# One encoder layer in full precision: the window of held operations opens at step 3, with a margin on TensorE

## The chip, the core and the metric

The kernel runs on one core of a Trainium2 chip. The core has five engines that each work through their own instruction stream in order: TensorE (PE: matmuls, and transposes done as matmuls), VectorE (DVE), ScalarE (ACT), GpSimd (POOL) and SyncE (SP, which here only issues DMAs). They wait for each other through semaphores. The metric is the time of one execution on the device, in microseconds.

## What is computed

One layer of a bidirectional encoder over 256 tokens with 4096 columns, in float32:

```python
h = rms_norm(x, g_mix)
proj = h @ w_in                      # 4096 x 11840: latents, rotary key, gates, q, k, v
y_a = mla_attention(...)             # 16 heads, low-rank q and kv, rotary part, dense softmax
y_b = dilated_mixture_attention(...) # 16 heads, three dilated windows with ALiBi, merged
x = x + concat(rms_norm(y_a, g) * silu(gate_a), rms_norm(y_b, g) * silu(gate_b)) @ w_out
x = x + (p @ w_ple) * sigmoid(rms_norm(x, g_ple) @ w_ple_gate)
out = rms_norm(x, g_final)
```

Nearly all of the work is five products of the 256 tokens with weights of 4096 rows (`w_in`, `w_out`, `w_ple_gate`) or fewer (`w_uq`, `w_ukv`). The weights are read once, about 365 MB.

## The kernel before

**Precision.** PE works on fp32r operands. To keep float32's precision each operand is split in a rounded part and a remainder: `hi` is a copy by ACT that rounds, `lo = src - hi` a subtraction by DVE (`split`, L415). A product is then three matmuls, hi x hi, hi x lo and lo x hi (`mm`, L433), accumulated in one PSUM bank. So each 512 KB piece of weights costs a load (SP), one ACT instruction, one DVE instruction and twelve matmuls of 512 columns.

**Steps.** The long products are cut into steps, one per 128 rows of weights and 1024 columns (`plain_step`), with some steps replaced by a Strassen-like scheme that forms sums of weights on DVE and saves one product in eight (`fast_steps`, letters a, b, g, h of `ORDER_*`). A step loads its weights into one of four raw slots, splits them into one of three pairs `hi`, `lo` (pool `wp`, and other tiles where they are free), and issues its matmuls into the eight PSUM banks m0 to m3, s, o, t0, t1. The main loop (L2232) goes through all steps: hooks, loads for some steps ahead (`fetch`), splits ahead (`convert`), the step's matmuls (`step.run`), and between them pieces of other tasks (`advance`): attention heads (`attend`), transposes of x, statistics, the epilogues of each product.

**The opening.** x comes in 512-column blocks (`load_x`, order 4, 5, 6, 7, 0 to 3). `x_turn` transposes a 128-token, 256-column piece on PE, and ACT and DVE scale it by the norm's gain and split it into `Ah`/`Al` (tiles A..h, A..l). Before the loop the program issues six small matmuls on a tile of zeros (`warm_up`), the transpose of the gains, the transposes of x block 8 into banks s and o (`x_turn(8, first)`), three more warm-up matmuls, and the splits of steps 0 and 1. Step 0 takes its weights in two halves; `blk.front` puts the split of its own piece of x ahead of the split of its weights. In step i of the first fifteen after step 0, `x_bank((i + 8) % 16)` transposes and splits the next piece of x, ahead of that step's matmuls.

**What sets the order.** All calls on an engine go through `Metered` (L253), which reckons a duration and hands the operation to two models. `clock` (class `Clock`) is a model of the engines in program order; the program asks it what to do next, and the change doesn't touch it. `window` (class `Window`, L179) holds operations back and issues them in another order: an operation is open when everything it depends on inside the window has been issued (`push`, L190); `step` (L221) takes for each engine the open operations that could start within `near` = 0.15 us of the earliest start by the window's own clock, and of these the first in program order; of the engines' candidates it issues the one that starts first. SP and POOL are kept in program order (`FIFO`). The window holds up to 200 operations:

```python
HELD = 200, 0.15                                              # L36
window = Window(*HELD)                                        # L327
at = max(free, min(op.at for op in ops))                      # L226
op = min((op for op in ops if op.at <= at + self.near), key=lambda op: op.nr)
```

`op.at` is the time at which the operation's operands are ready by the model. Operations are thus issued in an order fixed when the program is built; on the chip, every engine then follows its own list and waits wherever the next one isn't ready. Two matmuls that write overlapping parts of a PSUM tile keep their order by the dependency rule in `push`; two that write different parts of one tile (the transposes of one `tp`, the two halves of `s`) could be swapped.

All instructions are recorded at line 290, the helper that issues them, so the profile's groups are told apart by the names of tiles: m, s, o, t are the PSUM banks, `hi`, `lo` the split weights, `B`, `T`, `Ah`, `Al` tiles with several uses, `raw_all` the raw weights.

Of the kernel before, what the change touches and what calls it, by code (L numbers as in the profile page):

```python
# [32 lines left out]
SLOPES = [2.0 ** (-8.0 * (h + 1) / HEADS) for h in range(HEADS)]  # L33
FAR = 1e32
WARM = 6, 3
HELD = 200, 0.15  # L36
ORDER_D = (
    "cccccccccccccccccaccccbccccgchcccc",
    "ccccaabcbcgcgchhcaabbggcahchbagchbghcabgacbghhcc",
# [139 lines left out]
class Window:  # L179
# [10 lines left out]
    def push(self, engine, us, outs, ins, late, do, reads):  # L190
        op = Op(self.nr, engine, us, outs, ins, late, do)
        self.nr += 1
        first = set()
        if engine in self.FIFO and not getattr(self.tail.get(engine), "gone", True):
            first.add(self.tail[engine])
        self.tail[engine], op.gone = op, False
        for aps, wrote in ((reads, False), (outs, True)):
            for ap in aps:
                name, lo, hi = Clock.place(ap)
                both = wrote or ap.space == bass.MemoryType.PSUM  # L200
                for other, a, b, w in self.held.get(name, ()):
                    if (both or w) and a < hi and lo < b:
                        first.add(other)
                op.spans.append((name, lo, hi, both))
        for name, *span in op.spans:
            self.held.setdefault(name, []).append((op, *span))
        first.discard(op)
        op.before = len(first)
        for other in first:
            other.then.append(op)  # L210
        self.n += 1
        if not op.before:
            self.ready(op)
        while self.n > self.size:
            self.step()
# [5 lines left out]
    def step(self):  # L221
        best = None
        for engine, ops in self.open.items():
            if ops:
                free = self.clock.free[engine]
                at = max(free, min(op.at for op in ops))  # L226
                op = min((op for op in ops if op.at <= at + self.near), key=lambda op: op.nr)
                at = max(at, op.at)
                if best is None or (at, op.nr) < best[:2]:
                    best = at, op.nr, op  # L230
        op = best[2]
        self.open[op.engine].remove(op)
        op.gone = True
        self.n -= 1
        for name in {span[0] for span in op.spans}:
            self.held[name] = [h for h in self.held[name] if h[0] is not op]
        op.do()
        self.clock.run(op.engine, op.us, op.outs, op.ins, op.late)
        for other in op.then:
            other.before -= 1  # L240
            if not other.before:
                self.ready(other)
# [81 lines left out]
def encoder_layer(ctx: ExitStack, tc: tile.TileContext, x, p, positions, g_mix, w_in, g_q_latent, w_uq,  # L324
                  g_kv_latent, w_ukv, g_out_mla, g_out_dil, w_out, w_ple, g_ple, w_ple_gate, g_final,
                  c_inv, c_dist, out):
    whole, clock, window = tc.nc, Clock(), Window(*HELD)  # L327
    nc = Engines(whole, clock, window)
    x, p, out = x[0], p[0, 0], out[0]
    w_in, w_uq, w_ukv, w_out, w_ple, w_ple_gate = (w[0] for w in (w_in, w_uq, w_ukv, w_out, w_ple, w_ple_gate))  # L330
# [21 lines left out]
    def bank(tag, shape, bufs=1):  # L352
        names[tag] = names.get(tag, 0) + 1
        return made(lambda: pp.tile([P, *shape], F32, tag=tag, name=f"{tag}_{names[tag]}", bufs=bufs), tag, bufs)
# [55 lines left out]
    gone = set()  # L410
# [47 lines left out]
    G, at = {"mix": gT[:, :32]}, 0  # L458
# [69 lines left out]
    class Flags(set):  # L528
        at = {}
# [43 lines left out]
    def spawn(task, later=False, first=False):  # L573
        urgent.append(task)
        due[task] = 0.0
        if later:
            lazy.add(task)
        if first:
            hot.add(task)
# [17 lines left out]
    def advance(force=False, spare=True):  # L597
        if force:
            ahead = [due.get(t, 0.0) for pool in (urgent, running) for t in pool]
            now = clock.free["pe"]  # L600
            clock.free["pe"] = max(now, min([d for d in ahead if d > now], default=now))
        now = clock.free["pe"]
        if waiting and len(running) < 5 and now - begun[0] >= waiting[0][2] and waiting[0][0] <= flags:
            needs, task, _ = waiting.pop(0)
            running.append(task)
            due[task] = max([flags.at[f] for f in needs], default=0.0)
            begun[0] = now
        for pool in (urgent, running):
            for task in list(pool):
                if due.get(task, 0.0) <= clock.free["pe"] + SOON and (  # L610
                        force or task in hot or (spare or task not in lazy) and room() > ROOM):
                    resume(pool, task)
# [25 lines left out]
    def x_square(b):  # L638

        i, o = divmod(b, 2)  # L640
        nc.scalar.activation(xjunk[:, o], xs[i][:, o], AF.Square, accum_out=sq[:, o, i:i + 1])

    def x_bank(b):
        tp = turn_bank([2, S])
        x_turn(b, (tp[:, 0], tp[:, 1]))
        kts = slice(2 * b, 2 * b + 2)
        at = slice(2 * b % 8, 2 * b % 8 + 2)
        split_rows(*(q[:, at] for q in xT[b // 4]), tp, G["mix"][:, kts])
        x_square(b)
        flags.add(("x", b))  # L650
# [350 lines left out]
    def turn_steps(n, tags):  # L1001
# [36 lines left out]
        def done():  # L1038
# [27 lines left out]
            flags.add(("pe", n))  # L1066

        return [step(j) for j in range(4)]

    us, yT = {}, {}  # L1070
# [542 lines left out]
    def wide_ple(k):  # L1613
# [27 lines left out]
        def out():  # L1641
# [4 lines left out]
            yield  # L1646

        return [step(0), step(1)]

    def wide_mid(k, blk):  # L1650
# [315 lines left out]
    for n, (dil, half) in enumerate(((None, 0), (1, 0), (1, 1), (0, 0), (0, 1))):  # L1966
# [15 lines left out]
        free = {0: ("head", 1, HEADS - 1), 1: "turned q", 2: "turned q", 3: ("gated", 1, 3), 4: ("gated", 1, 3)}[n]  # L1982
        allow(blk, "B4", lambda i, n=n, f=free, end=mid_step: f in flags and (n % 2 == 1 or i < end))
        free = {0: "kv", 1: "kv"}.get(n, ("gated", 1, 1))
# [91 lines left out]
    for c in range(8):  # L2076
        at = fast[G_AT[c // 4]] + 1 + 2 * (c % 4)
# [20 lines left out]
    class Old(Step):  # L2098
# [9 lines left out]
        def fetch(self):  # L2108
            ch, j, i = self.ch, self.j, self.i
            self.slots.append(raw_slot())  # L2110
            raw[i] = raw_tile(self.slots[0], (ch.per, ch.n))
            w, at = ch.per * P, ch.row(j)
            nc.sync.dma_start(raw[i], ch.src[w * at:w * (at + 1), :].rearrange("(k p) n -> p k n", p=P))
# [59 lines left out]
    def convert_one(upto):  # L2173
        if converted[0] >= min(upto, len(steps)):
            return False
        i = converted[0]
        fetch(i + 1)
        assert fetched[0] > i
        st = steps[i]
        if not all(f in flags for f in st.holds):  # L2180
            return False
        got = st.halves() or tiles(i, st)
        if got is None:
            return False
        hi, lo = got
        st.split(hi, lo)
        halves[i] = hi, lo
        if st.frees:
            raw_release(st.slots)
        converted[0] += 1  # L2190
        fetch(upto + 3)
        return True

    def convert(upto):
        while convert_one(upto):
            pass

    def slack(i):

        c = converted[0]  # L2200
        if c >= len(steps):
            return 1e9
        need = clock.free["pe"] + sum(steps[k].time for k in range(i + 1, c))
        return need - max(clock.free["dve"], clock.free["pe"])
# [21 lines left out]
    first = [bank(tag, [S]) for tag in ("s", "o")]  # L2226
# [3 lines left out]
    warm_up(WARM[1])  # L2230
    convert(AHEAD)
    for i, step in enumerate(steps):  # L2232
        if i in hooks:
            for f in hooks[i]:
                f()
        if i < 16 and i % 2 == 0 and 3 + i // 2 < 8:
            next(loads[3 + i // 2])
        lead = i + AHEAD + (7 if i > wide_end - 4 else 3 if len(step.ring) > 3 else 0)
        fetch(lead + 3)
        if i < START:  # L2240
            if 0 < i < 16:
                x_bank((i + 8) % 16)
            if i == 2:
                x_square(8)
            convert(lead + 1)
        n = 0
        while not all(f in flags for f in step.needs) or any(b in locks for b in step.banks) or i not in halves:
            advance(True)
            convert(lead + 1)
            n += 1  # L2250
            assert n < 200, (i, step.needs)
        step_end[0] = clock.free["pe"] + step.time
        step.run(*halves.pop(i))
        ran[0] = i
        if step.after:
            spawn(step.after(), first=step.mid)
            if step.ahead:
                urgent.insert(0, urgent.pop())
            advance()
        while slack(i) < MARGIN and convert_one(lead + 1):  # L2260
            pass
        advance(spare=slack(i) > MARGIN)
        convert(lead + 1)
# [24 lines left out]
```

## Time and profile before

| | us |
|---|---|
| median of 3 runs | 1895.77 (1894.84 to 1895.93) |
| the profiled execution, its time | 1896.45 |
| its span, first to last instruction | 1894.7 |
| PE busy | 1875.6 (99%) |
| DVE busy | 1685.9 (89%) |
| ACT busy | 1164.7 (61%) |
| POOL busy | 31.7 (2%) |

The mean granted clock of TensorE is 0.996 of full speed, and DMA moves 196 GB/s on average. The profile is of one execution. Its page gives busy times, the span in forty slices, the chain that ended last and the costliest groups. Besides the page, the trace answers: the waits of an engine (who waited for whom), the busy time of each engine in given stretches with the granted clock beside it, and the instructions in order of time. A row in order of time reads: start, duration, engine, line, operation, out<-in by the program's names, shape, count, and in brackets the idle time of the engine before it with what ended that. A PE matmul's end is modelled: its shown duration is longer than its distance to the next one.

### The profile page before, as it was taken

What the parts mean: (1) busy time and instruction counts of PE and PEld (TensorE: products, weight loads), DVE (VectorE), ACT (ScalarE), POOL (GpSimd) and SP (SyncE); (2) the same over time, 40 slices, a digit from 0 to 9 for tenths busy, and PEclk for the clock granted to TensorE, in tenths of its full rate; (3) what the DMA queues carried; (4) which work ended last, traced back from release to release, by engine and by line L of the source; (5) the groups of instructions that cost most, each with busy time, mean ns of one, the idle gap of its engine ahead of it and who ended that gap; (6) DMA issues with size and microseconds to landing.
All of it is one profiled execution on the core that took longest, in us unless ns stands there. A gap on an engine that the chain in (4) does not pass through costs nothing.

```text
span 1894.7 us, 25419 instructions
## 1 busy us (share of the span) xinstructions
PE 1875.6 (99%) x9130; PEld 1583.1 (84%) x9130; DVE 1685.9 (89%) x2278; ACT 1164.7 (61%) x1570; POOL 31.7 (2%) x41
## 2 busy tenths in 40 slices
PE   8999999999999999999999999999999999999997
PEld 6888888888899888888888999888888888888886
DVE  5999999989989889899898777889888989999997
ACT  6656566555688665666556666656555556666654
POOL 0000000000001000000000010100000000000000
PEclk9999999999999999999999999999999999999999
DMA  7756666666735556576667554566566566666665
GB/s 268 222 191 210 200 206 203 194 205 214 215 90 152 167 191 201 187 215 196 222 186 207 142 142 135 167 226 213 195 217 219 172 209 212 202 219 199 201 219 192
DMA packets 160872, 370.58 MB, mean 196 GB/s; under 512 B 29117, under 2 KB 70953, under 8 KB 160745
## 3 DMA queue, kind: packets, MB, share of 16 engines
q1 hardware_dynamic: 159896, 366.58, 60.9%
q0 software_dynamic: 512, 1.84, 0.3%
q8 instruction: 71, 1.16, 0.3%
q10 hardware_dynamic: 336, 0.54, 0.1%
q14 instruction: 57, 0.46, 0.1%
HBM read 364.72 MB, written 4.19 MB: 195 GB/s over the span
## 4 chain that ended last, share of the span: by engine, by line
PE 68%; DVE 2%; ACT 1%; issue 0%; DVEq 0%; ACTq 0%
PE m L290 40%; PE t L290 12%; PE s L290 9%; PE o L290 8%; DVE T L290 1%; ACT T L290 0%; DVE lo L290 0%; DVE st L290 0%; ACT Ah L290 0%; DVE B L290 0%; DVE Ah L290 0%; ACT hi L290 0%; ACT B L290 0%; ACT L290 0%; ACT Q L290 0%
## 5 line engine op out<-in xcount | busy, mean ns | idle before, releaser
L290 ACT ACTIVATE hi<-raw_all 128x1024 fp32r<-128x1024 f32 (+2 forms) x419 | 416.9, 999 | 281.4 <-PE m L290 81.3
L290 DVE TENSOR_TENSOR lo<-raw_all,hi 128x1024 fp32r<-128x1024 f32 (+2 forms) x419 | 479.6, 1151 | 85.8 <-ACT hi L290 82.6
L290 PE MATMUL m<-hi,Ah 128*128 128x512 f32 (+2 forms) x722 | 269.6, 388 | 0.0
L290 PE MATMUL m<-hi,Al 128*128 128x512 f32 (+2 forms) x648 | 239.9, 382 | 0.0
L290 PE MATMUL m<-lo,Ah 128*128 128x512 f32 (+2 forms) x593 | 225.5, 380 | 0.0
L290 ACT ACTIVATE B<-raw_all 128x1024 fp32r<-128x1024 f32 (+2 forms) x146 | 143.9, 989 | 96.0 <-PE m L290 25.7
L290 DVE TENSOR_TENSOR B<-raw_all,B 128x1024 fp32r<-128x1024 f32 (+2 forms) x146 | 166.0, 1140 | 18.1 <-ACT B L290 17.4
L290 DVE TENSOR_TENSOR raw_all<-raw_all 128x512 f32<-128x512 f32 (+1 forms) x229 | 164.6, 721 | 4.8 <-DMA raw_all<-in_w_out_dram 1.1
L290 PE MATMUL m<-hi,B 128*128 128x512 f32 (+1 forms) x486 | 166.5, 390 | 0.0
L290 PEld LDWEIGHTS m<-hi,Ah 128*128 128x128 f32 x722 | 136.5, 189 | 24.6
L290 PEld LDWEIGHTS m<-hi,Al 128*128 128x128 f32 x648 | 122.4, 189 | 23.0
L290 PE MATMUL m<-B,Ah 128*128 128x512 f32 (+2 forms) x535 | 141.4, 357 | 0.0
L290 PEld LDWEIGHTS m<-lo,Ah 128*128 128x128 f32 x593 | 112.3, 189 | 19.2
L290 PEld LDWEIGHTS m<-hi,B 128*128 128x128 f32 x486 | 91.1, 188 | 18.1
L290 PEld LDWEIGHTS m<-B,Ah 128*128 128x128 f32 x535 | 92.6, 189 | 13.5
L290 PE MATMUL m<-B,Al 128*128 128x512 f32 (+2 forms) x293 | 100.0, 372 | 0.0
L290 PE MATMUL m<-lo,B 128*128 128x512 f32 (+1 forms) x243 | 94.3, 388 | 0.0
L290 PE MATMUL t<-hi,Ah 128*128 128x512 f32 x218 | 82.5, 391 | 0.0
L290 ACT ACTIVATE hi<-B 128x1024 fp32r<-128x1024 f32 (+1 forms) x57 | 56.5, 996 | 37.1 <-PE t L290 11.8
L290 DVE TENSOR_TENSOR lo<-B,hi 128x1024 fp32r<-128x1024 f32 (+1 forms) x57 | 65.1, 1146 | 3.5 <-ACT hi L290 2.9
L290 PE MATMUL t<-lo,Ah 128*128 128x512 f32 x168 | 65.4, 389 | 0.0
L290 PEld LDWEIGHTS m<-B,Al 128*128 128x128 f32 x293 | 55.0, 188 | 9.5 <-DVE B L290 0.3
(495 smaller groups left out, 4171.8 us busy)
## 6 DMA issues: line engine op xcount, KB each, us to landing
raw_all<-in_w_in_dram SPq DMA_DIRECT2D x258, 512.0 KB, 4.4
raw_all<-in_w_out_dram SPq DMA_DIRECT2D x100, 512.0 KB, 4.5
raw_all<-in_w_ple_gate_dram SPq DMA_DIRECT2D x90, 512.0 KB, 5.0
T<-in_w_in_dram SPq DMA_DIRECT2D x59, 512.0 KB, 4.4
B<-in_w_in_dram SPq DMA_DIRECT2D x42, 512.0 KB, 4.3
Ah<-in_w_ple_gate_dram SPq DMA_DIRECT2D x38, 512.0 KB, 5.1
raw_all<-in_w_uq_dram SPq DMA_DIRECT2D x48, 256.0 KB, 3.2
B<-in_w_out_dram SPq DMA_DIRECT2D x18, 512.0 KB, 4.7
```

Of the source, the lines that this page charges most:

```text
L290: self.window.push(key, us, outs, ins, late, lambda: do(out, *rest, **named), reads)
```

## The change

Three things are changed in the scheduler; what is computed and which instructions are issued stay the same.

- The window starts with size 0, so that each operation is issued at once, in program order. When the main loop reaches step 3 (`OPENING`), its size becomes 200, as it was.
- In `step`, a margin `SAFE` of 0.8 us is added to the ready times of PE's open operations when candidates are chosen: the earliest possible start is reckoned with the margin, and an operation counts as a candidate only if its ready time plus the margin lies within `near` of that. Other engines have a margin of 0. The time at which the chosen operation is then said to start is reckoned without the margin.
- In `push`, operations of PE that write the same PSUM tile are chained in program order, as SP's and POOL's are. Across tiles they may still pass each other.

```diff
-HELD = 200, 0.15
+HELD, OPENING, NEAREST = 200, 3, 0.15
+SAFE = {"pe": 0.8}
...
-        if engine in self.FIFO and not getattr(self.tail.get(engine), "gone", True):
-            first.add(self.tail[engine])
-        self.tail[engine], op.gone = op, False
+        line = engine if engine in self.FIFO else (engine, outs[0].name) if engine == "pe" else None
+        if line and not getattr(self.tail.get(line), "gone", True):
+            first.add(self.tail[line])
+        self.tail[line], op.gone = op, False
...
-                at = max(free, min(op.at for op in ops))
-                op = min((op for op in ops if op.at <= at + self.near), key=lambda op: op.nr)
-                at = max(at, op.at)
+                safe = SAFE.get(engine, 0.0)
+                at = max(free, min(op.at for op in ops) + safe)
+                op = min((op for op in ops if op.at + safe <= at + self.near), key=lambda op: op.nr)
+                at = max(free, op.at)
...
-    whole, clock, window = tc.nc, Clock(), Window(*HELD)
+    whole, clock, window = tc.nc, Clock(), Window(0, NEAREST)
...
     for i, step in enumerate(steps):
+        if i == OPENING:
+            window.size = HELD
```

## The prediction

> **What bounds the kernel now.** I start with the page's first part, because one engine near 100% decides what a reordering can be worth at all; then the waits of TensorE (PE), longest first.
>
> ```profile
> span 1894.7 us, 25419 instructions
> PE   1875.6 (99%) x9130; PEld 1583.1 (84%) x9130; DVE 1685.9 (89%) x2278; ACT 1164.7 (61%) x1570; POOL 31.7 (2%) x41
> ...
> PE t L290 <- DMA T<-in_x_dram: 3.3, 1, 3.3
> PE m L290 <- DVE junk L290: 1.5, 1, 1.5
> PE s L290 <- DVE T L290: 1.2, 3, 0.7
> PE s L290 <- ACT T L290: 0.4, 1, 0.4
> ```
>
> PE is busy for all but 19.1 us of the span, and only 6.4 us of that is waiting for something: 3.3 us once for an x block, 1.5 us at the very start for the warm-up tile, and 1.6 us in four waits of attention's scores (bank s). The other 12.7 us lie behind the last matmul. A busy PE need not be a PE at its peak, so the second view is the busy time by stretch (columns: PE, PEld, DVE, ACT, POOL, then granted clock, DMA share, GB/s).
>
> ```profile
> 0.00:10.00 10.00, 5.20 (x19) 2.48 (x19) 2.86 (x5) 4.39 (x8) 0.73 (x7) 0.91 0.78 260
> 10.00:20.00 10.00, 10.00 (x38) 8.04 (x37) 5.15 (x8) 7.30 (x16) 0.00 (x0) 0.75 0.96 364
> ...
> 100.00:200.00 100.00, 100.00 (x443) 82.85 (x442) 93.97 (x109) 58.95 (x68) 0.00 (x0) 1.00 0.60 203
> ...
> 500.00:600.00 100.00, 98.79 (x724) 95.31 (x723) 88.82 (x174) 80.13 (x161) 9.92 (x11) 1.00 0.48 141
> ...
> 1000.00:1100.00 100.00, 99.61 (x644) 90.99 (x643) 78.90 (x109) 61.35 (x97) 1.88 (x2) 1.00 0.62 170
> ```
>
> From 100 to 200 us, 443 matmuls fill 100 us: one each 0.226 us, the same pitch that two neighbours show at full clock below (15.15 and 15.38). So in the long stages PE is saturated; the change removes no matmul, and nothing is to be won there by order. What order can win is the first 15 us, where PE stands idle and then runs at reduced clock (0.91 and 0.75: 0.9 + 2.5 = 3.4 us lost, which is 6.8 us at half speed), and the few holes of attention, in the last two rows' stretches. The opening in order of time:
>
> ```profile
> 4.13 0.31 PE L290 MATMUL t<-ident,T 32*128 32x32 f32 x1
> ...
> 4.37 1.03 PE L290 MATMUL m<-junk 128*128 128x512 bf16 x3
> 4.47 0.20 ACT L290 ACTIVATE gT<-t 128x32 f32<-128x32 f32 x1 [1.97 <-PE t L290]
> 4.70 0.63 ACT L290 ACTIVATE hi<-raw_all 128x512 fp32r<-128x512 f32 x1
> ...
> 5.24 0.27 PE L290 MATMUL s<-ident,T 128*128 128x128 f32 x1
> ...
> 7.11 0.63 ACT L290 ACTIVATE hi<-raw_all 128x512 fp32r<-128x512 f32 x1 [1.78 <-DMA raw_all<-in_w_in_dram]
> 7.77 0.69 DVE L290 TENSOR_TENSOR lo<-raw_all,hi 128x512 fp32r<-128x512 f32 x1 [1.72 <-ACT hi L290]
> 8.35 1.15 ACT L290 ACTIVATE hi<-raw_all 128x512 fp32r<-128x512 f32 x2 [0.61 <-DMA raw_all<-in_w_in_dram]
> ...
> 9.01 1.29 DVE L290 TENSOR_TENSOR lo<-raw_all,hi 128x512 fp32r<-128x512 f32 x2 [0.55 <-ACT hi L290]
> ...
> 9.19 1.09 PE L290 MATMUL t<-ident,T 128*128 128x128 f32 x4 [3.34 <-DMA T<-in_x_dram]
> ...
> 9.40 0.46 ACT L290 ACTIVATE Ah<-s,gT 128x256 fp32r<-128x256 f32 x1
> 9.76 0.46 ACT L290 ACTIVATE Ah<-o,gT 128x256 fp32r<-128x256 f32 x1
> ...
> 9.93 0.78 PE L290 MATMUL m<-hi,Ah 128*128 128x512 f32 x1
> ...
> 10.69 1.05 ACT L290 ACTIVATE hi<-raw_all 128x1024 fp32r<-128x1024 f32 x1
> ...
> 14.34 0.63 PE L290 MATMUL m<-lo,Ah 128*128 128x512 f32 x1
> ...
> 14.77 0.54 PE L290 MATMUL m<-hi,Al 128*128 128x512 f32 x1
> ...
> 15.15 0.40 PE L290 MATMUL m<-hi,Ah 128*128 128x512 f32 x1
> ...
> 15.38 0.40 PE L290 MATMUL m<-lo,Ah 128*128 128x512 f32 x1
> ...
> 17.89 0.60 PE L290 MATMUL t<-ident,T 128*128 128x128 f32 x4
> 18.24 0.48 PE L290 MATMUL m<-hi,Ah 128*128 128x512 f32 x1
> ```
>
> The reader is to see an order that is not the program's. In the program `x_turn(8)` (the transposes into s and o) stands ahead of the second warm-up, step 0's operand `Ah<-s` ahead of all halves of weights, and step 0's products ahead of the transposes of `x_bank(9)`. On the chip the reverse was issued: the transposes come behind the warm-up (5.24 behind 4.37), `Ah<-s` behind four halves that wait for weights (9.40 behind 8.35), and `x_bank(9)`'s transposes ahead of step 0 (9.19 ahead of 9.93), where they hold PE for 3.34 us until x has landed. PE then does step 0's twelve products from 9.93 to 15.15 at 0.43 us each (14.34 to 14.77), and step 1's twelve from 15.15 to 17.89 at 0.23.
>
> **Part 1: the first three steps in program order.** `Window(0, ...)` issues each operation as it is pushed. Nothing is added or removed; three engines' orders change, SP's and POOL's are FIFO both ways. The chain by these rows: warm-up and gains transpose as now, to 4.37. x's first half-block must be there; the view of tile T in the first microsecond has it:
>
> ```profile
> DMA to landing us min/median/max: 2.4/2.6/2.8
> ```
>
> Two loads, issued at 0.74, so landed by 3.6: no wait. Four transposes at 0.11 to 0.21 us, the two of s done by about 5.0; `Ah<-s` at 5.1; ACT starts its next instruction 0.36 later (9.40 to 9.76), so the first half of step 0's weights is rounded 5.5 to 6.1 (its data was there at 4.70), its remainder on DVE 6.2 to 6.9 (0.69). PE: first product 6.2 instead of 9.93, the second waits for the remainder until 7.0, six are done by 8.1. The other half stays bound by its load: rounded at 7.11, remainder done 7.77 + 0.69 = 8.46; so the eighth product starts at 8.5 and the twelfth is done at 8.5 + 5 x 0.23 = 9.65. Then `x_bank(9)`'s transposes, whose data was there at 9.19: 0.35 us (17.89 to 18.24), to 10.0. Step 1's halves are finished at 10.3 now (9.01 + 1.29) and some 0.1 to 0.3 later with `Al<-o` put ahead of them: step 1 runs from 10.0 to 12.8 at full clock. Now it ends at 17.89. **Lead: 17.89 - 12.8 = 5.1 us**, of which about 2.6 is the clock (13 products at 0.43 instead of 0.23) and the rest the idle time. Step 2 is the thin spot: its weights are rounded at 10.69 now, behind it come `x_bank(9)`'s two roundings, and DVE's remainders follow; I make it ready at 13.1, PE arrives at 12.8 + 0.35. A miss there costs about 0.3.
>
> Whether the lead holds to the end depends on the same row as always: PE is 100% busy from 10 us on, so whatever it starts earlier stays earlier unless weights or DVE come late. The loads' pace is 364 GB/s in the second ten microseconds, 1.44 us for 512 KB, and a step of PE takes 2.7 plus 0.35; and splits wait for buffers that PE frees, so they move along.
>
> **Part 2: TensorE lets others pass one just become ready (0.8), and one bank's matmuls keep their order.** The first is a margin against a time that was reckoned too early. Where it pays:
>
> ```profile
> 519.22 0.28 PE L290 MATMUL m<-B,Al 128*128 128x256 f32 x1
> 519.34 0.28 PE L290 MATMUL s<-T 128*128 128x256 f32 x1
> 519.96 0.86 PE L290 MATMUL s<-T 128*128 128x256 f32 x5 [0.34 <-DVE T L290]
> ...
> 584.97 0.95 PE L290 MATMUL s<-T 128*128 128x256 f32 x6 [0.70 <-DVE T L290]
> ```
>
> The hole at 519.34 is really 0.62 - 0.12 = 0.50 us, since the shown end of a matmul lies 0.16 behind the next one's start (0.28 against a pitch of 0.12, from 519.22 to 519.34). So the four score waits cost 1.6 + 4 x 0.16 = 2.2 us. Gain between 0 and 2.2. Cost: each operation of a head's chain on PE can come 0.65 us later (0.8 less 0.15), covered as long as other matmuls are collected; below nothing it is the rival further down. I take 1.2, half of what is there, nearest to the waits of 0.3 to 0.5 us that a margin of 0.65 covers whole. The bank rule forbids swaps inside one PSUM tile alone; accumulations were ordered already, so only transposes and a pair's halves lose a freedom that nothing in PE's saturated rows uses: 0.
>
> The tail (12.7 us) is a chain of DVE and ACT behind the last matmul; no part of the change orders it: 0.
>
> **Sum.** The profiled execution took 1896.45 us (span 1894.7), 0.7 above the median of 1895.77. 1896.45 - 5.1 - 1.2 = 1890.15; from the median, 1889.5.
>
> **The rivals.**
>
> *The clock falls back* (0.2). Now the clock is down until about 15.1, so from about 8.3 on (6.8 us at half speed), though PE was idle only from 5.85 to 9.19 (3.34 us); in the new order PE has two holes of 0.4 to 0.5 us before 8.1, so I expect it to stay up. If it falls all the same for half of the 6.8 us, 3.4 x 0.5 = 1.7 us of the lead are lost: 1896.45 - 3.4 - 1.2, or 1891.2 from the median. The Trainium skill ("TensorE: Matmul & The Clock Gate", Part 1) says that the clock is halved after at least one idle window of about 3.4 us, with free-running windows. By that rule the new order keeps its clock and the 5.1 stands; the trace here agrees only in part, since the clock fell with an idle stretch of 3.34 us that filled no whole window, some 2.4 us after the last transpose.
>
> *DVE gives the lead back* (0.15).
>
> ```profile
> 60.00:70.00 10.00, 10.00 (x47) 8.31 (x46) 9.90 (x17) 6.52 (x9) 0.00 (x0) 1.00 0.80 254
> 70.00:80.00 10.00, 10.00 (x45) 8.26 (x44) 9.86 (x22) 5.73 (x7) 0.00 (x0) 1.00 0.59 174
> 80.00:90.00 10.00, 10.00 (x46) 8.28 (x45) 9.83 (x24) 4.54 (x6) 0.00 (x0) 1.00 0.74 211
> 90.00:100.00 10.00, 10.00 (x46) 8.29 (x45) 9.66 (x22) 8.06 (x12) 0.00 (x0) 1.00 0.62 184
> ```
>
> From 60 to 100 DVE has 0.75 us to spare. If its sums of x start no earlier than now, PE waits there until its lead is down to about 1: 1895.8 - 1 - 1.2 = 1893.6. Against it: DVE is idle for 12 of the first 20 us, so its work can move forward with PE's.
>
> *The margin starves attention* (0.1; the other side). Each of 32 heads passes PE four times; if PE has nothing else collected when a delayed operation is held, 0.65 us show each time. Sixteen such holes eat the 6.3 us and 3.8 more; one for every head gives 1895.8 - 5.1 + 32 x 0.65 = 1911.5. For it: 500 to 600 us is the stretch with the least cover (98.79 busy). Against: a held operation is taken at once when no other is open.
>
> *Nothing moves* (0.05): the new order equals the old. The rows at 9.40 and 9.19 speak against it. 1895.8.
>
> **How the numbers follow.** Forecast 0.5: 1889.5, between 1888.0 (all 2.2 us, and 5.5) and 1891. 0.2% is 3.8 us, about what a measurement of this kernel can tell from no change: below 1892.0 is faster, above 1899.6 slower. Faster: the forecast and two thirds of the clock's case, 0.64. Slower: the starved heads, 0.10. Same: 0.26. The range goes from 1887.0, a little under the floor of the sum, to 1897.0, which takes in the clock, DVE and nothing moved, and leaves out the starved heads.
>
> **What would show it.** Right: the first m product near 6.2 us, no wait of PE for T<-in_x_dram, PEclk near 1.0 in the second ten microseconds, the transposes now at 17.89 near 13; fewer than four waits of s. Wrong: a half clock between 8 and 12 us (first rival), PE holes behind DVE between 40 and 120 us (second), new waits of t, s or o of some 0.6 us between 500 and 600 or 1050 and 1200 (third). The last matmul must end some 6 us earlier, with the tail at 12.7.

## The result, and the profile after

| | before | changed |
|---|---|---|
| median of 8 runs each, us | 1895.95 (1894.84 to 1896.65) | 1890.38 (1889.71 to 1891.13) |
| span of the profiled execution, us | 1894.7 | 1888.8 |
| PE busy, us | 1875.6 | 1873.0 |

The ratio is 0.9971, 95% interval 0.9960 to 0.9982: faster by 5.6 us, or 0.29%. Forecast was 1889.5. The waits of PE in the changed kernel (columns: total us, times, longest):

```profile
PE m L293 <- DVE junk L293: 1.5, 1, 1.5
PE s L293 <- DVE T L293: 0.5, 1, 0.5
PE m L293 <- DVE Ah L293: 0.4, 1, 0.4
PE s L293 <- ACT T L293: 0.4, 1, 0.4
PE m L293 <- DVE lo L293: 0.2, 1, 0.2
```

The 3.3 us for T<-in_x_dram are gone, and of the score waits 1.6 us became 0.9. A wait for Ah is new. The busy time by stretch, with the same columns as before:

```profile
0.00:10.00 10.00, 8.19 (x31) 4.69 (x32) 4.02 (x7) 4.79 (x9) 0.74 (x7) 1.00 0.81 267
10.00:20.00 10.00, 10.00 (x52) 8.24 (x51) 7.24 (x10) 9.81 (x23) 0.00 (x0) 1.00 1.04 407
500.00:600.00 100.00, 99.45 (x733) 96.26 (x732) 90.05 (x186) 81.56 (x170) 9.76 (x11) 1.00 0.46 134
1000.00:1100.00 100.00, 99.61 (x666) 91.90 (x665) 77.62 (x112) 63.12 (x103) 2.62 (x3) 1.00 0.61 167
```

The matmuls of the second ten microseconds, 52 for 38, say more than the busy time, which is 10.00 both times. Most of the gain is there before 20 us are over. The opening in order of time:

```profile
5.16 0.47 ACT L293 ACTIVATE Ah<-s,gT 128x256 fp32r<-128x256 f32 x1 [0.49 <-PE s L293]
5.27 0.81 PE L293 MATMUL m<-junk 128*128 128x512 bf16 x3
...
5.53 1.29 ACT L293 ACTIVATE hi<-raw_all 128x512 fp32r<-128x512 f32 x2
...
6.21 0.49 PE L293 MATMUL m<-hi,Ah 128*128 128x512 f32 x1
...
6.93 0.50 PE L293 MATMUL m<-lo,Ah 128*128 128x512 f32 x1 [0.23 <-DVE lo L293]
...
9.56 0.60 PE L293 MATMUL t<-ident,T 128*128 128x128 f32 x4
...
12.78 0.60 PE L293 MATMUL t<-ident,T 128*128 128x128 f32 x4
13.13 0.48 PE L293 MATMUL m<-hi,Ah 128*128 128x512 f32 x1
```

The transposes that follow step 1 start at 12.78; before they started at 17.89. The lead in these two executions is 5.1 us, and the span is shorter by 5.9. The last matmuls, before (L290) and after (L293):

```profile
1881.52 0.52 PE L290 MATMUL m<-Ah,B 128*128 128x256 f32 x3
1875.70 0.52 PE L293 MATMUL m<-Ah,B 128*128 128x256 f32 x3
```

They start 5.8 us earlier, and the tail behind them stays at 12.6 to 12.7 us.

### The profile page after: what moved, and what is told of

The parts are those of the page before. It is cut to its first block, busy times and chain, and to the rows that moved or that the text cites. A ratio compares the mean times of both kernels' runs of the same rounds, so it can differ in the third digit from the quotient of the medians.

```text
span 1888.8 us, 25423 instructions
## 1 busy us (share of the span) xinstructions
PE 1873.0 (99%) x9130; PEld 1581.2 (84%) x9130; DVE 1686.2 (89%) x2278; ACT 1165.5 (62%) x1570; POOL 30.9 (2%) x41
## 4 chain that ended last, share of the span: by engine, by line
PE 93%; DVE 4%; ACT 1%; DMA 1%; issue 1%; SPq 0%; DVEq 0%; ACTq 0%
PE m L293 53%; PE t L293 18%; PE s L293 12%; PE o L293 10%; DVE T L293 2%; DVE lo L293 1%; DMA raw_all<-in_w_ple_gate_dram 1%; DVE B L293 0%; ACT hi L293 0%; DVE Ah L293 0%; ACT T L293 0%; ACT Ah L293 0%; DVE st L293 0%; DMA B<-in_g_final_dram 0%; DVE raw_all L293 0%
## 5 line engine op out<-in xcount | busy, mean ns | idle before, releaser
L293 ACT ACTIVATE hi<-raw_all 128x1024 fp32r<-128x1024 f32 (+2 forms) x419 | 417.0, 999 | 276.6 <-PE m L293 80.2
L293 DVE TENSOR_TENSOR lo<-raw_all,hi 128x1024 fp32r<-128x1024 f32 (+2 forms) x419 | 479.7, 1151 | 79.5 <-ACT hi L293 75.8
L293 PE MATMUL m<-hi,Ah 128*128 128x512 f32 (+2 forms) x722 | 268.4, 386 | 0.1
L293 PE MATMUL m<-hi,Al 128*128 128x512 f32 (+2 forms) x648 | 239.0, 380 | 0.0
L293 PE MATMUL m<-lo,Ah 128*128 128x512 f32 (+2 forms) x593 | 224.7, 379 | 0.2 <-DVE lo L293 0.2
L293 ACT ACTIVATE B<-raw_all 128x1024 fp32r<-128x1024 f32 (+2 forms) x146 | 143.8, 989 | 96.2 <-PE m L293 25.0
L293 DVE TENSOR_TENSOR B<-raw_all,B 128x1024 fp32r<-128x1024 f32 (+2 forms) x146 | 165.2, 1134 | 18.0 <-ACT B L293 17.2
L293 DVE TENSOR_TENSOR raw_all<-raw_all 128x512 f32<-128x512 f32 (+1 forms) x229 | 164.2, 719 | 3.9 <-DMA raw_all<-in_w_out_dram 1.1
L293 PE MATMUL m<-hi,B 128*128 128x512 f32 (+1 forms) x486 | 166.4, 389 | 0.0
L293 PEld LDWEIGHTS m<-hi,Ah 128*128 128x128 f32 x722 | 135.8, 188 | 25.0 <-ACT hi L293 0.6
L293 PE MATMUL m<-B,Ah 128*128 128x512 f32 (+2 forms) x535 | 142.3, 358 | 0.0
L293 PEld LDWEIGHTS m<-hi,Al 128*128 128x128 f32 x648 | 121.8, 188 | 22.6
L293 PEld LDWEIGHTS m<-lo,Ah 128*128 128x128 f32 x593 | 111.7, 188 | 19.6 <-DVE lo L293 0.5
L293 PEld LDWEIGHTS m<-hi,B 128*128 128x128 f32 x486 | 91.1, 188 | 18.0
L293 PEld LDWEIGHTS m<-B,Ah 128*128 128x128 f32 x535 | 92.9, 189 | 13.6
L293 PE MATMUL m<-B,Al 128*128 128x512 f32 (+2 forms) x293 | 99.8, 371 | 0.0
L293 PE MATMUL m<-lo,B 128*128 128x512 f32 (+1 forms) x243 | 94.2, 388 | 0.0
L293 PE MATMUL t<-hi,Ah 128*128 128x512 f32 x218 | 82.5, 391 | 0.0
L293 ACT ACTIVATE hi<-B 128x1024 fp32r<-128x1024 f32 (+1 forms) x57 | 56.5, 996 | 36.3 <-PE t L293 11.8
L293 DVE TENSOR_TENSOR lo<-B,hi 128x1024 fp32r<-128x1024 f32 (+1 forms) x57 | 65.0, 1145 | 3.6 <-ACT hi L293 3.0
L293 PE MATMUL t<-lo,Ah 128*128 128x512 f32 x168 | 65.4, 389 | 0.0
L293 PEld LDWEIGHTS m<-B,Al 128*128 128x128 f32 x293 | 55.1, 188 | 9.2
```

What stands on the lines that cost most here:

```text
L293: self.window.push(key, us, outs, ins, late, lambda: do(out, *rest, **named), reads)
```

## The experiments

Each was run beside the kernel before on the same chip; a ratio is that of the experiment to it. Three chips were used (e1 to e4, e5 to e8, e9 to e12), so medians of different groups are compared less surely than those within one. The margin without the bank rule (e3) has no time: in that order a matmul starts a new sum in bank s while another sum there is unfinished, and would spoil it. So the margin's effect was measured only together with the bank rule.

**One part at a time.** e1 keeps only the opening, e2 only the margin and the bank rule, e4 only the bank rule.

```diff
# e1_opening_only
-SAFE = {"pe": 0.8}
+SAFE = {}
-        line = engine if engine in self.FIFO else (engine, outs[0].name) if engine == "pe" else None
+        line = engine if engine in self.FIFO else None
# e2_margin_and_bank
-    whole, clock, window = tc.nc, Clock(), Window(0, NEAREST)
+    whole, clock, window = tc.nc, Clock(), Window(HELD, NEAREST)
# e4_bank_only: as e2_margin_and_bank, and
-SAFE = {"pe": 0.8}
+SAFE = {}
```

> The window opens at step 3, without the margin and without the bank rule. Theory A (the opening's order carries the gain): the opening's own lead of 5.1 us, so 1896.0 - 5.1 = 1890.9, first m product near 6.2 us, PEclk 1.0 in the second ten microseconds, and the score holes of before (0.3 to 0.9 us) still there. Theory B (the margin on PE carries it): within 1 us of before, 1895 to 1896.5. Theory C (the opening's order needs the bank rule, so that a pair of products isn't interleaved): 1892 to 1894.

> Margin and bank rule with the window at 200 from the first operation on. Theory A: 0 to 1.2 us below before, 1894.8 to 1896.0, with the 3.3 us wait for T<-in_x_dram and the half clock still there. Theory B: 1890 to 1892. The margin could also mend the opening by itself, since a late x block is held 0.8 us longer: then the wait would be gone and the time 1891 to 1893.

> The bank rule alone, window at 200 from the first operation on, no margin. Theory A: no change, 1895.3 to 1896.5, holes of PE as before. If the bank rule matters, more than 1 us either way.

The kernel before had a median of 1896.36 us beside these.

| | median, us | ratio, 95% interval |
|---|---|---|
| e1, opening only | 1892.00 (1891.43 to 1893.65) | 0.9978 (0.9969 to 0.9987) |
| e2, margin and bank rule | 1894.80 (1893.54 to 1896.41) | 0.9991 (0.9982 to 1.0000) |
| e4, bank rule | 1896.67 (1895.06 to 1898.23) | 1.0002 (0.9993 to 1.0012) |

The opening alone brings 4.4 us. The margin and the bank rule bring 1.6, with an interval that touches 1, so this run doesn't show it by itself; the bank rule alone brings nothing that can be measured. Theory B falls: with the opening's order alone the time is 4.4 us down. Theory C falls by the trace and not by the median, which lies at the edge of its range (1892 to 1894): step 1 is done at 12.87 us in e1, as with the bank rule (12.78). That the margin mends the opening by itself falls too; here is what PE waits for in e2:

```profile
PE t L293 <- DMA T<-in_x_dram: 2.2, 1, 2.2
PE m L293 <- DVE junk L293: 1.5, 1, 1.5
PE s L293 <- DVE T L293: 0.5, 1, 0.5
PE s L293 <- ACT T L293: 0.4, 1, 0.4
```

and in e1:

```profile
PE m L293 <- DVE junk L293: 1.5, 1, 1.5
PE s L293 <- DVE T L293: 0.9, 2, 0.7
PE s L293 <- ACT T L293: 0.4, 1, 0.4
```

The margin alone doesn't take the x wait away; the opening's order does. But that wait is not all that held step 0 back. In the kernel before ACT wrote `Ah<-s`, the first products' operand, only at 9.40, behind roundings that waited for weights, although the last transpose of its source started at 5.46. The transposes that wait for x and this operand were both done near 9.9, so by these rows mending PE's order alone could hardly have brought the first product forward. In the changed kernel ACT does `Ah<-s` at 5.16. No run changes one of the two orders without the other.

The margin takes some of the score waits: 1.6 us before, 1.3 with the opening alone, 0.9 with the margin. One execution each says little about 0.4 us: second profiles, further down, list 1.4 for the kernel before and 1.2 for the changed one.

**How much of the lead is the clock?** e8 profiles the kernel before once more; e6 gives it more warm-up matmuls, so that PE isn't idle while it waits for x; e5 takes all warm-up from the changed kernel.

```diff
# e6_before_more_warm_up (the kernel before)
-WARM = 6, 3
+WARM = 6, 15
# e5_after_no_warm_up (the changed kernel)
-WARM = 6, 3
+WARM = 0, 0
```

> The kernel before, profiled once more, to see what changes from one execution to another. The half clock lies between 4.8 and 20 us at another place, or is shorter; the holes of the scores near 519, 526, 584 and 1067 us are the same; the last loads of w_ple_gate take 5.0 to 6.6 us and PE waits for them for 0 to 1 us near 1862 to 1869 us.

> The kernel before with 15 instead of 3 matmuls in the second warm-up (twelve more, 2.6 us at full clock, which fill most of the idle 3.3 us). Theory A with the clock as half of it: the clock stays at full speed through step 0, so 2 to 3 us are saved without any change of order: 1893.3 to 1894.4. If the order alone is the gain, no change, 1896.4, or slower by what the warm-up delays.

> The changed kernel without its nine warm-up matmuls. If the clock carries half of the lead (2.6 of 5.1 us), step 0's products run at 0.43 us each until a window of 3.4 us has been busy: 1.5 to 3 us slower than the changed kernel, 1892 to 1893.4, with PEclk under 1.0 in the first twenty microseconds. If the lead is all idle time removed, no difference: 1890.4.

The kernel before, a second time, PE in order of time:

```profile
8.84 0.79 PE L290 MATMUL t<-ident,T 128*128 128x128 f32 x4 [2.55 <-DMA T<-in_x_dram]
9.44 0.79 PE L290 MATMUL m<-hi,Ah 128*128 128x512 f32 x1
...
11.74 0.63 PE L290 MATMUL m<-hi,Al 128*128 128x512 f32 x1
12.16 0.59 PE L290 MATMUL m<-hi,Ah 128*128 128x512 f32 x1
12.59 0.40 PE L290 MATMUL m<-lo,Ah 128*128 128x512 f32 x1
12.83 0.39 PE L290 MATMUL m<-hi,Al 128*128 128x512 f32 x1
...
16.50 0.60 PE L290 MATMUL t<-ident,T 128*128 128x128 f32 x4
```

and its stretches:

```profile
0.00:10.00 10.00, 5.99 (x19) 2.77 (x20) 3.33 (x6) 4.75 (x9) 0.73 (x7) 0.96 0.76 260
10.00:20.00 10.00, 10.00 (x43) 8.05 (x42) 5.87 (x9) 6.90 (x16) 0.00 (x0) 0.87 1.03 411
```

Its four score waits lie at the same places. The same program is done with step 1 at 16.50 in one execution and at 17.89 in the other: the transposes that wait for x start 0.35 us sooner (8.84 for 9.19), and seven products instead of twelve run at 0.43 us (the pitch turns between 12.16 and 12.83; the prediction counted thirteen in the first execution, but its rows show the twelve of step 0). The half clock, 0.4 + 1.3 = 1.7 us of loss, is 3.4 us long here and was 6.8. So the lead over this execution is 16.50 - 12.78 = 3.7 us, not 5.1. Two more executions, e2 and e4, begin with the window open like the kernel before; their transposes behind step 1:

```profile
17.29 0.60 PE L293 MATMUL t<-ident,T 128*128 128x128 f32 x4
16.15 0.60 PE L293 MATMUL t<-ident,T 128*128 128x128 f32 x4
```

The leads over the four are 5.1, 4.5, 3.7 and 3.4 us, 4.2 on average. Against the 4.4 by which e1's median is lower this fits; the 5.1 was the largest of them.

e6 came to 1894.67 (1892.85 to 1895.39), ratio 0.9992 (0.9983 to 1.0001), beside a median of 1896.17 for the kernel before: 1.5 us, less than the 2 to 3 expected, and about the 1.7 that a half clock of 3.4 us costs; an interval that touches 1 doesn't show it by itself. PE in e6:

```profile
9.15 0.60 PE L290 MATMUL t<-ident,T 128*128 128x128 f32 x4
9.84 0.50 PE L290 MATMUL m<-hi,Ah 128*128 128x512 f32 x1
10.18 0.40 PE L290 MATMUL m<-lo,Ah 128*128 128x512 f32 x1
...
15.43 0.60 PE L290 MATMUL t<-ident,T 128*128 128x128 f32 x4
```

This separates the two halves, in single executions. The first product is as late as before (9.84 for 9.93), but all run at full clock, and step 1 is done at 15.43. What is left to 12.78, 2.65 us, is order alone; 17.89 - 15.43 = 2.5 us in the one execution and 16.50 - 15.43 = 1.1 in the other is the clock's share, give or take the 0.3 us by which x lands sooner or later.

e5 came to 1891.80 (1890.79 to 1892.73), ratio 0.9978 (0.9970 to 0.9987): 1.4 us above the changed kernel's median (1.2 when each is taken from its own kernel before), a little under the 1.5 to 3 expected, and the two intervals overlap. Its trace shows the mechanism: the products start 0.43 us apart until 9.32 (8.05 to 8.48, say), though the clock column shows 1.00, and step 1 is done at 13.45 for 12.78. PE starts step 0 sooner without the warm-up in its way (5.45 for 6.21) and wins back a part.

**The margin's size.** 1.6 us for 0.8 in e7; then e10 and e11 (2.4 us) beside e9, the changed kernel again; e12 opens the window at step 12.

```diff
# e7_margin_1_6, e10_margin_1_6_again (e11_margin_2_4: 2.4)
-SAFE = {"pe": 0.8}
+SAFE = {"pe": 1.6}
# e12_opening_12
-HELD, OPENING, NEAREST = 200, 3, 0.15
+HELD, OPENING, NEAREST = 200, 12, 0.15
```

> The changed kernel with a margin of 1.6 us for 0.8. Theory A: the holes of 0.7 and 0.5 us that the margin of 0.8 left (at about 578 and 1061 us of the changed kernel) go, 1 us at most: 1889.3 to 1890.4. The rival of starved heads: a longer margin delays each head's four passes by another 0.8 us, so new waits of t, s or o appear: 1891 to 1900.

> The changed kernel again, beside the two margins below on one chip: 1890 to 1891. A hole of PE near 1862 us, where it waits for the last loads, of another size than the first time (0 to 1.3 us), if that hole is a matter of the execution and not of the change.

> Margin 1.6 us again: if the longer margin is worth the two holes that it closed (0.7 near 578 and 0.55 near 1061 us), 1.0 to 1.3 us below e9_changed_again; if its lead was a matter of chips and rounds, within 0.4 us of it.

> Margin 2.4 us. With no score hole left at 1.6 there is nothing to win: as e10_margin_1_6_again. If a long margin starves the heads' chains, new waits of t, s or o and 1 us or more above it.

> The window opens at step 12 for 3, the rest as in the changed kernel. Theory A: steps 0 to 2 are all that the model of the engines got wrong, so no difference to e9_changed_again (within 0.5 us), unless the program's own order makes PE wait for roundings between steps 3 and 11: then 0.5 to 2 us slower. If the reckoned order is wrong further on, faster by more than 0.5 us.

| | median, us | ratio, 95% interval |
|---|---|---|
| e7, margin 1.6 | 1889.17 (1889.14 to 1891.36) | 0.9967 (0.9954 to 0.9979) |
| e9, margin 0.8 | 1890.33 (1889.97 to 1891.97) | 0.9974 (0.9964 to 0.9984) |
| e10, margin 1.6 | 1889.20 (1888.88 to 1889.27) | 0.9966 (0.9954 to 0.9979) |
| e11, margin 2.4 | 1890.37 (1890.03 to 1892.06) | 0.9974 (0.9964 to 0.9984) |
| e12, opening 12 | 1891.08 (1890.16 to 1892.35) | 0.9974 (0.9965 to 0.9984) |

At 1.6 us the kernel is 1.1 us faster than the changed one beside it; the single runs don't overlap, the intervals against the kernel before do. In e7 the attention stretches have no hole left:

```profile
500.00:600.00 100.00, 100.00 (x736) 96.64 (x734) 89.43 (x186) 81.80 (x170) 9.69 (x11) 1.00 0.45 136
1000.00:1100.00 100.00, 100.00 (x669) 92.36 (x668) 78.20 (x114) 64.07 (x104) 2.62 (x3) 1.00 0.62 169
```

A margin of 0.8 had left the larger holes, as here in the changed kernel:

```profile
578.12 0.31 PE L293 MATMUL m<-lo,Ah 128*128 128x320 f32 x1
578.97 0.71 PE L293 MATMUL s<-T 128*128 128x256 f32 x4 [0.55 <-DVE T L293]
```

The scores start 0.85 us after a matmul whose pitch is 0.15 (578.12 to 578.97; the one ahead of it started at 577.97): 0.70 us lost, after 0.8 of margin. If the margin held these scores back here, their operand was reckoned over 1 us too early (0.65 and 0.70, an estimate); that the hole is gone at 1.6 agrees. At 2.4 us the rival that I had priced for 0.8 appears, in e11:

```profile
530.61 0.27 PE L293 MATMUL t<-ident,B7a 128*128 128x128 f32 x1
531.38 0.39 PE L293 MATMUL o<-T,T 128*128 128x256 f32 x1 [0.50 <-ACT T L293]
531.86 0.38 PE L293 MATMUL s<-T 128*128 128x256 f32 x1
```

A hole ahead of an o product, one of a head's own chain: 0.77 us for a transpose of 0.11, so 0.66. It isn't the whole 1.2 us by which e11 is slower than e10: e11's last matmuls start only 0.4 us later (1874.53 for 1874.11), and the other 0.7 us of its span lie in the tail of DVE and ACT behind them, for a reason that stays open. e12 is 0.75 us above e9 with runs that overlap: no difference shown, so program order beyond step 2 buys nothing, and whether it costs stays open. In its profile step 1 is done at 13.25 for 12.78, in steps whose order is the changed kernel's.

**The new wait for Ah** near 1862 us: PE waits there for the split of the last weights. The wait of 0.4 us in the first profile of the changed kernel has no counterpart in its second, whose waits are

```profile
PE m L293 <- DVE junk L293: 1.5, 1, 1.5
PE s L293 <- ACT T L293: 0.7, 2, 0.4
PE s L293 <- DVE T L293: 0.5, 1, 0.5
PE m L293 <- DVE lo L293: 0.2, 1, 0.2
```

So it comes and goes from one execution of this kernel to another.

## Why the prediction was right, point by point

**The order of the opening was read rightly.** First product at 6.2: 6.21. Second held by its remainder until 7.0: 6.93. `x_bank(9)`'s transposes at 9.65: 9.56. Step 1 done at 12.8: 12.78. Step 2, the thin spot, started at 13.13 without a wait. One link differs: the second half of the weights, which I kept bound by its load until 7.11, had landed sooner here and followed the first half without a wait (two at 5.53). That is luck of the execution: in e1 it was rounded at 7.01 and in e12 at 7.35, and in e12 the eighth product waited for it until 8.76. The chain of the prediction mends both orders that held step 0 back, PE's and ACT's; one alone would not have done.

**The lead's size came from the slowest opening.** 5.1 us is what the two profiles show, and 4.4 is what the opening brings in the medians (2.5 to 5.9 by the interval, so 5.1 is not excluded). The term that is probably mis-sized is the clock's: read from one execution with 6.8 us of half clock, whose twelve products at 0.43 us make 2.4 us. A second one has seven, and its lead would be 3.7. The rest held: 2.5 us in the sum, 2.65 against e6.

**The margin's gain, 1.2 us of 2.2, is not shown to that accuracy.** Margin and bank rule bring 1.6 us alone (up to 3.4 or nothing by the interval), and the changed kernel is 1.2 us further below its kernel before than e1 is. In the traces less is seen: PE's busy time between 500 and 600 us goes from 98.79 to 99.45, and in the second executions of the two kernels from 98.95 to 99.18. I had said that a margin of 0.65 covers the waits of 0.3 to 0.5 us whole. It covered the two near 519 and 526 us (the second execution of the changed kernel has one of 0.27 near 515); the hole at 578 us stays, as does the wait of 0.39 us near 1062, and the stretch from 1000 to 1100 us is busy for 99.61 as before. The bank rule was worth 0 in time, as put, but the margin needs it.

**The rivals.** The clock did not fall back: 52 matmuls in the second ten microseconds, and step 1's twelve products with their transposes done in 3.2 us (9.56 to 12.78). DVE did not give the lead back, though it is as full as feared:

```profile
50.00:60.00 10.00, 10.00 (x49) 8.21 (x49) 10.00 (x19) 7.76 (x13) 0.00 (x0) 1.00 0.73 235
60.00:70.00 10.00, 10.00 (x46) 8.28 (x45) 9.83 (x20) 4.99 (x6) 0.00 (x0) 1.00 0.71 222
```

PE has no hole there; the trace lists none between 20 and 578 us. DVE's work moved forward with PE's: of the first 40 us DVE was idle for 19.2 before and for 14.1 after, 5.1 less, which is the lead. The starved heads did not appear at 0.8; one such hole does at 2.4. Most of the span's difference is accounted for: 5.1 in the opening and 0.7 between 500 and 600 us, less 0.4 for the new wait near 1862 us, are 5.4 of 5.9; some 0.5 us of gain are not assigned to a place.

## What to carry to other kernels

Where one engine is busy 99% of a span, look for the first microseconds in which it isn't, and compare the order that was issued with the order of the program: here a reckoned order put PE's transposes that wait for x ahead of the first products, and ACT's roundings that wait for weights ahead of those products' operand, for a loss that nothing later made up. Look at the order of every engine that feeds the first work, not only of the one that idles. A list scheduler that works with a model of the chip wants a margin on the engine that mustn't stop, of the size of the model's error and no more (0.8 left holes, 1.6 closed them, 2.4 made one). Before a term is sized from a stretch at reduced clock, profile a second execution.

## What was not expected of the hardware

The length of the half clock is a matter of the execution: 6.8 us in one profile of the kernel before and 3.4 in another, with idle times of PE of 3.3 and 2.6 us ahead of it. The Trainium skill ("TensorE: Matmul & The Clock Gate", Part 1) speaks of free-running windows of about 3.4 us, and both lengths are whole numbers of such windows. Its rule that the clock falls after at least one idle window doesn't cover what is seen here: 2.6 us idle were enough. In the longer case PE was still idle for the first 0.9 us of the half clock (8.3 to 9.19), in the shorter it was busy nearly throughout (about 9.2 to 12.6); whether that makes the difference is not shown.

The granted clock of the profile can be too high at the start. In e2 the second stretch shows 1.00:

```profile
10.00:20.00 10.00, 10.00 (x38) 8.04 (x38) 5.51 (x9) 7.08 (x15) 0.00 (x0) 1.00 1.03 399
```

yet only 38 matmuls fit, as many as in the first profile of the kernel before (52 after the change), and they start 0.43 us apart until 14.11:

```profile
11.54 0.63 PE L293 MATMUL m<-hi,Ah 128*128 128x512 f32 x1
11.97 0.63 PE L293 MATMUL m<-lo,Ah 128*128 128x512 f32 x1
...
14.11 0.40 PE L293 MATMUL m<-lo,Ah 128*128 128x512 f32 x1
14.35 0.39 PE L293 MATMUL m<-hi,Al 128*128 128x512 f32 x1
```

At the start of a span the pitch of the matmuls tells the clock, not the column.
